# Fourier and attention layers on one core: squares of the shared weight tiles by pieces, separate load buffers, another pace for the modulation

## The chip, the cores and the metric

The kernel runs on one core of a Trainium2 chip. A core has TensorE (PE, matrix products), VectorE (DVE), ScalarE (ACT), GpSimd (POOL) and SyncE (SP, which only issues transfers here). The metric is the device time of one execution in microseconds (us); lower is better.

## The reference

Two layers work on 256 tokens and 256 context tokens of width 2048. Layer 0 mixes by a Fourier transform, layer 1 by attention. Each has a modulation (shift, scale, gate) out of `c`, and an output product `y @ w_out`.

```python
def _fourier_branch(h, w_in, w_mix):
    b, n, _ = h.shape
    u, z = jnp.split(h @ w_in, 2, axis=-1)
    ug = u.reshape(b, n, FNET_GROUPS, FNET_GROUP_DIM).astype(jnp.float32)
    f = jnp.fft.fft2(ug, axes=(1, 3), norm='ortho').real.astype(h.dtype)
    f = jnp.einsum('bngc,gcd->bngd', f, w_mix).reshape(b, n, D_BRANCH)
    return f * jax.nn.silu(z)
...
    for i in range(DEPTH):
        shift, scale, gate = jnp.split((jax.nn.silu(c) @ ada_w[i] + ada_b[i])[:, None, :], 3, axis=-1)
        h = _rmsnorm(x, norm_g[i]) * (1 + scale) + shift
        if need_ctx or kind == 1:
            shift_c, scale_c, gate_c = jnp.split(jax.nn.silu(c_ctx) @ ada_w[i] + ada_b[i], 3)
            hc = _rmsnorm(xc, norm_g[i]) * (1 + scale_c) + shift_c
        if kind == 0:
            y = _fourier_branch(h, fnet_w_in[j], fnet_w_mix[j])
            yc = _fourier_branch(hc, fnet_w_in[j], fnet_w_mix[j]) if need_ctx else None
        elif kind == 1:
            y, yc = _attention_branch(h, hc, attn_w_in[j], attn_sink[j], rows, cols, need_ctx)
...
        x = x + gate * (y @ w_out[i])
        if need_ctx:
            xc = xc + gate_c * (yc @ w_out[i])
    return _rmsnorm(x, final_g)
```

## The kernel before

Tokens and context tokens are handled together, as 512 columns. The stages in order of time, with the profile's times:

- **Opening** (to some 120 us): norm, modulation of layer 0, and the Fourier transform over the tokens.
- **u-stage** (to some 337 us): 16 groups `g` of the Fourier branch. For each group two tiles `wu` of 1 MB come from memory, are folded on DVE (L134, L140), split into a high and a low part on ACT (L66) and DVE (L67), and multiplied with the tokens held in 32 `act` tiles; the mix matrix `m` comes through ACT's queue. The result `ft` goes to a table `fd` in memory.
- **z-stage** (to some 672 us): the other half of `w_in`. The first four output blocks, b = 0 to 3, share four tiles `wz0` (one per four k, loop over `kg`); each of blocks 4 to 31 has a tile `wz` of its own. A tile is first squared and summed over (`squares`, L161), the sum gives a scale (`total` on POOL, `scale`), and then it is split into two half-precision tiles `w16` (`split16`: ACT L179, then DVE L180). A block is 48 matmuls: 16 k, three products each (L79, L80, L81). The tokens `hs` are built anew for each k by `make_hs` (DVE L768, ACT L769, DVE L770). `z_out` takes the Silu of the block (ACT L779) and multiplies it with the branch tile `ys[b]`, read back from `fd`.
- **Output product of layer 0, wo0** (to some 1008 us): 32 tiles, n = 0 to 31, each 48 matmuls again, in the order of the list `outs`. `y_split` makes the halves of y; `evac0` scales the result by `gd`, the gate times the tile's scale, and adds it to x.
- **Layer 1**: attention, to the end.

Beside the z-stage and wo0 run the 64 **modulation steps** (`ada_step`): a step loads one tile `adw` of 1 MB and forms four sums on DVE (L730, output `junk`), two for the last 16 steps. The `cb` vectors they use have their Silu on ACT (L723).

The order of the work on each engine is not written by hand. A scheduler takes the program's order, the buffers of the pools and hints (`tc.issue_after`) and fixes one sequence for each engine; an engine then takes its instructions strictly in that sequence. So a buffer that is not free, or an instruction whose input is late, holds back all that follows on its engine or queue. All loads of weights go through SP's queue.

The pools that matter: `rawp` with three buffers of 1 MB (`raw`); `zp`, three more (`rawz`), whose memory is free only after the u-stage's pools have closed; `wsp` with six buffers for split weights; `actp` with 33 buffers, of which the tokens take 32 in the u-stage; eight PSUM banks. `raw6` takes `raw` and `rawz` in turn, for weights and `adw` alike. `fetch(n)` loads, squares and scales tile n; `weights(n)` splits it and calls `fetch(n + 2)`.

Of the kernel before, what the change touches and what calls it, by code (L numbers as in the profile page):

```python
# [32 lines left out]
def tile_dit(ctx: ExitStack, tc: tile.TileContext, a: dict, out: bass.AP):  # L33
# [13 lines left out]
    def raw(src, q=None):  # L47
        t = rawp.tile([P, D], F32, tag="raw", name="raw")
        n = src.shape[-1]
        last_dma[0] = (q or nc.sync).dma_start(t[:, :n], src).ins  # L50
        return t
# [108 lines left out]
    def squares(dump, src, col, scale=1.0):  # L160
        sq_ins[0] = S.activation(dump, src, AF.Square, scale=scale, accum_out=col).ins  # L161
# [407 lines left out]
        fill_pe(len(fill))  # L569


    w4 = adap.tile([P, 4], F32, name="w4")
    hsc = adap.tile([P, 2, KT, 2], F32, name="hsc")
    hq = [small("hq") for _ in range(3)]
    squares(hsc[:, 0], gs0, hq[0], 64.0)
# [16 lines left out]
    for g in range(G):  # L592
# [36 lines left out]
        if g == 13:  # L629
            w1 = small("w1", bufs=1)  # L630
            V.tensor_reduce(w1, w4, axis=AX.X, op=ALU.add)
            u4, d4 = scale(total(w1), hdn, "4", 1)
        if 8 <= g < 12:
            t = raw(a["wz0"][g - 8])
            squares(t, t, w4[:, g - 8 : g - 7])
        if g > 4:
            with tc.issue_after(m_end[2]):
                w.append({"m": split_part("m", f3[1][1])})
# [99 lines left out]


    adat = lay0.enter_context(tc.tile_pool(name="adat", bufs=1))  # L740
    junk = adat.tile([P, 1056], BF16, name="junk")[:, 0:1024]
    acc = adat.tile([P, 4, 2, KT, 2], F32, name="acc")
    YA = 8
    with tc.tile_pool(name="yp", reuse_waits="tile", bufs=33 - YA) as ypool, tc.tile_pool(name="zp", reuse_waits="tile", bufs=3) as zp:
        ys = [act() if b < YA else ypool.tile([P, 512], F32, tag="y", name="y") for b in range(NB)]
        hs = []
        hs_end = [None] * 3
        turn = [0]

        def raw6(src, view=lambda t, s: ((t, s),)):  # L750
            turn[0] += 1
            pool, nm = (rawp, "raw") if turn[0] % 2 else (zp, "rawz")
            t = pool.tile([P, D], F32, tag=nm, name=nm)
            for d, s in view(t, src):
                last_dma[0] = nc.sync.dma_start(d, s).ins
            return t

        ada_raw = raw6

        def make_hs(k):  # L760
            xt = act()
# [9 lines left out]
            hs.append((hl[:, 0:512], hl[:, 512:1024]))  # L771

        yq = adap.tile([P, NB], F32, name="yq")
        yup, ydn, yy = [None] * 2, [None] * 2, []

        def z_out(b, o, dn):
# [25 lines left out]
        def fetch(n):  # L802
            if n >= len(jobs):
                return
            nm, at_, i = jobs[n]
            if nm == "wz":
                t = raw6(a["wz"][at_])
            else:
                v = a["wo0"][at_[0] // 8, i * 8 : i * 8 + 8].rearrange("g p (j b f) -> p g j b f", j=2, b=8)[:, :, :, at_[0] % 8]
                t = raw6(v, lambda t, s: [(t.rearrange("p (g j f) -> p g j f", g=8, j=2)[:, :, j], s[:, :, j]) for j in range(2)])  # L810
            h, q = half16(), small("wq")
            squares(h, t, q)
            ready[n] = t, h, *scale(total(q), hdn if nm == "wz" else ydn[i])

        def weights(n):
            t, wh, up_, dn = ready.pop(n)
# [4 lines left out]

        o4 = [psum() for _ in range(4)]
        for kg in range(4):
            wr = raw6(a["wz0"][kg])
            wh, wl = half16(), half16()
            for i in range(2):
                make_hs(kg * 4 + i * 2)
                q = slice(i * 1024, (i + 1) * 1024)
                with tc.issue_after(hs_end[0]) if kg else nullcontext(), tc.issue_after(hs_end[1]) if kg else nullcontext():
                    split16(wh[:, q], wl[:, q], wr[:, q], u4)  # L830
                make_hs(kg * 4 + i * 2 + 1)
            for j in range(4):
                k = kg * 4 + j
                for b in range(4):
                    q = slice(j * 512 + b * P, j * 512 + (b + 1) * P)
                    mm3(o4[b], wh[:, q], wl[:, q], hs[k][0], hs[k][1], k == 0, k == KT - 1)
        for b in range(4):
            with tc.issue_after(last_dma[0]):
                nc.sync.dma_start(ys[b], fd[b])
        for b in range(4):  # L840
            z_out(b, o4[b], d4)
        fetch(0)
        fetch(1)
        for b in range(4, NB):
            wh, wl, dn = weights(b - 4)
            with tc.issue_after(last_dma[0]):
                nc.sync.dma_start(ys[b], fd[b])
            o = psum()
            for k in range(KT):
                q = slice(k * P, (k + 1) * P)  # L850
                mm3(o, wh[:, q], wl[:, q], hs[k][0], hs[k][1], k == 0, k == KT - 1)
            z_out(b, o, dn)
            if b == 15:
                y_scale(0)
            if b >= 16:
                y_split()
            with tc.issue_after(hs_end[0]) if b < 8 else nullcontext():
                ada_step(1)
# [4 lines left out]
        def evac0(b, i, o, dn):  # L863
            t = xin[b]
            gd = adap.tile([P, 2], F32, tag="gd", name="gd", bufs=4)
            V.tensor_scalar(gd, gt0[:, b, :], dn, None, op0=ALU.mult)
            t2 = act() if i else None
            for s in range(2):
                q = slice(s * N, (s + 1) * N)
# [19 lines left out]
        for n, (b, i) in enumerate(outs):  # L889
            if n == 0:  # L890
                y_scale(1)
            wh, wl, dn = weights(n + NB - 4)
            if n < 4:
                for _ in range(4):
# [5 lines left out]
            if n == 31:  # L900
                wr = raw(a["wkv"][0])
                w0 = half_split(wr, 0)
            ada_step(0 if n > 29 else 2 if n > 19 else 1)
            o = psum()
            for k in range(16):
                q = slice(k * P, (k + 1) * P)
# [631 lines left out]
```

## Time and profile before

| | us |
|---|---|
| median of 3 runs | 1787.43 (1785.95 to 1788.46) |
| profiled execution | 1785.5 |
| its span | 1783.7 |
| TensorE busy | 1731.1 (97%) |
| VectorE busy | 1398.2 (78%) |
| ScalarE busy | 1039.3 (58%) |

The span is the time from the first to the last recorded instruction of the profiled execution. In rows of waits the columns are: who waited, for whom, us in total, times, longest. In rows of the timeline: start, duration, engine and source line, operation, output<-input, count, and in brackets the idle time before it with the one that ended it. In rows of windows: the stretch, its length, then busy time and instruction count of PE, PEld (weight loads of TensorE), DVE, ACT and POOL, the granted clock of TensorE, the busy share of the DMA engines and GB/s.

### The profile page before, as it was taken

What the parts mean: (1) busy time and instruction counts of PE and PEld (TensorE: products, weight loads), DVE (VectorE), ACT (ScalarE), POOL (GpSimd) and SP (SyncE); (2) the same over time, 40 slices, a digit from 0 to 9 for tenths busy, and PEclk for the clock granted to TensorE, in tenths of its full rate; (3) what the DMA queues carried; (4) which work ended last, traced back from release to release, by engine and by line L of the source; (5) the groups of instructions that cost most, each with busy time, mean ns of one, the idle gap of its engine ahead of it and who ended that gap; (6) DMA issues with size and microseconds to landing.
All of it is one profiled execution on the core that took longest, in us unless ns stands there. A gap on an engine that the chain in (4) does not pass through costs nothing. (4 is left out here: it accounts for less than half of the span.)

```text
span 1783.7 us, 25965 instructions
## 1 busy us (share of the span) xinstructions
PE 1731.1 (97%) x9449; PEld 1204.6 (68%) x9449; DVE 1398.2 (78%) x2415; ACT 1039.3 (58%) x1708; POOL 256.6 (14%) x277
## 2 busy tenths in 40 slices
PE   6999999999999999999999999999999999999997
PEld 4679999644444444444444588788888888887886
DVE  5779778789889997953587463989999999997455
ACT  5544544485565656444334343777888888887343
POOL 0002111211000001100101000322212212234001
PEclk9999999999999999999999999999999999999999
DMA  9998898857777798654468323578898988888554
GB/s 393 417 340 230 234 279 237 288 214 283 275 261 264 259 327 256 204 164 130 131 226 275 112 97 104 174 179 219 213 208 211 216 208 208 210 216 262 197 179 142
DMA packets 267777, 403.06 MB, mean 226 GB/s; under 512 B 152641, under 2 KB 218577, under 8 KB 236161
## 3 DMA queue, kind: packets, MB, share of 16 engines
q1 hardware_dynamic: 243584, 363.39, 64.9%
q0 software_dynamic: 19920, 31.06, 6.9%
q10 hardware_dynamic: 4144, 6.95, 1.2%
q8 instruction: 74, 1.21, 0.3%
q14 instruction: 55, 0.44, 0.1%
HBM read 356.26 MB, written 12.59 MB: 207 GB/s over the span
## 5 line engine op out<-in xcount | busy, mean ns | idle before, releaser
L67 DVE TENSOR_TENSOR wl<-raw,wh 128x1024 fp32r<-128x1024 f32 x205 | 272.3, 1334 | 112.0 <-ACT wh L66 109.3
L66 ACT CAST wh<-raw 128x1024 fp32r<-128x1024 f32 x205 | 214.2, 1046 | 136.9 <-PE ps L80 123.6
L730 DVE CUSTOM_DVE_ANT_0 junk<-rawz,cb 128x1024 bf16<-128x1024 f32 x200 | 244.0, 1220 | 8.5 <-ACT cb L723 5.6
L80 PE MATMUL ps<-act,w 128*128 128x512 f16 x640 | 243.5, 381 | 0.5 <-DVE act L770 0.5
L79 PE MATMUL ps<-act,w 128*128 128x512 f16 x640 | 239.4, 381 | 4.0 <-ACT w L179 2.2
L81 PE MATMUL ps<-act,w 128*128 128x512 f16 x640 | 239.6, 379 | 0.2 <-DVE w L180 0.2
L1203 PE MATMUL ps<-h,wh 128*128 128x512 f32 x512 | 187.1, 403 | 0.0
L81 PEld LDWEIGHTS <-w 128*128 128x128 f16 x1024 | 100.2, 98 | 127.9 <-DVE w L180 6.8
L79 PEld LDWEIGHTS <-w 128*128 128x128 f16 x1024 | 100.4, 98 | 125.2 <-ACT w L179 3.3
L80 PEld LDWEIGHTS <-w 128*128 128x128 f16 x1024 | 100.4, 98 | 120.6 <-issue 0.8
L180 DVE SCALAR_TENSOR_TENSOR w<-raw,up,w 128x2048 f16<-128x2048 f32 (+1 forms) x58 | 131.8, 2274 | 51.5 <-PE ps L80 45.1
L161 ACT ACTIVATE w<-raw 128x2048 f16<-128x2048 f32 x54 | 102.8, 1904 | 94.2 <-PE ps L81 50.0
L81 PE MATMUL ps<-y,w 128*128 128x512 f16 x384 | 145.2, 379 | 4.0 <-DVE w L180 4.0
L80 PE MATMUL ps<-y,w 128*128 128x512 f16 x384 | 145.4, 379 | 0.0
L79 PE MATMUL ps<-y,w 128*128 128x512 f16 x384 | 144.9, 379 | 0.0
L1205 PE MATMUL ps<-h,wl 128*128 128x256 f32 x512 | 138.4, 281 | 0.0
L179 ACT ACTIVATE w<-raw,up 128x2048 f16<-128x2048 f32 (+1 forms) x58 | 112.1, 1935 | 23.3 <-DVE up L170 22.2
L80 PE MATMUL ps<-wl,h 128*128 128x512 f32 x320 | 125.1, 391 | 0.3 <-DVE wl L67 0.3
L81 PE MATMUL ps<-wh,h 128*128 128x512 f32 x320 | 123.8, 390 | 0.0
L79 PE MATMUL ps<-wh,h 128*128 128x512 f32 x320 | 122.4, 397 | 0.0
L165 POOL PARTITION_ALL_REDUCE tot<-wq x60 | 42.6, 713 | 541.5 <-ACT w L161 456.8
L1257 DVE SCALAR_TENSOR_TENSOR f<-p,sm,f 128x512 f16<-128x512 f32 x128 | 103.1, 824 | 12.0 <-ACT f L1256 11.8
(380 smaller groups left out, 4051.7 us busy)
## 6 DMA issues: line engine op xcount, KB each, us to landing
raw<-in_wz SPq DMA_DIRECT2D x65, 1024.0 KB, 5.3
rawz<-in_adw SPq DMA_DIRECT2D x56, 1024.0 KB, 5.1
raw<-in_awp SPq DMA_DIRECT2D x32, 1024.0 KB, 12.8
raw<-in_wq SPq DMA_DIRECT2D x32, 1024.0 KB, 5.2
raw<-in_wu SPq DMA_DIRECT2D x32, 1016.0 KB, 7.3
raw<-in_wo SPq DMA_DIRECT2D x54, 512.0 KB, 5.7
raw<-in_wo1b SPq DMA_DIRECT2D x16, 1024.0 KB, 4.9
act<-in_xT POOLq DMA_DIRECT2D x32, 256.0 KB, 6.3
```

The source lines that it names most:

```text
L66: last_cast[0] = S.copy(h, src).ins
L67: last_sub[0] = eng.tensor_tensor(l, src, h.bitcast(F32), op=ALU.subtract).ins
L79: PE.matmul(o, wh, xh, start=start, stop=False)
L80: PE.matmul(o, wh, xl, start=False, stop=False)
L81: return PE.matmul(o, wl, xh, start=False, stop=stop).ins
L161: sq_ins[0] = S.activation(dump, src, AF.Square, scale=scale, accum_out=col).ins
L179: last_cast[0] = S.activation(h, src, AF.Copy, scale=up).ins
L180: last_sub[0] = V.scalar_tensor_tensor(l, src, up, h, op0=ALU.mult, op1=ALU.subtract).ins
L730: V.tensor_tensor_reduce(junk, wf, cb[:, s], 1.0, 0.0, ALU.mult, ALU.add, acc[:, i, kh, fg * 2 + f, s : s + 1])
L1203: PE.matmul(o[0], wh[:, q], hx1[k], start=k == 0, stop=k == KT - 1)
L1205: PE.matmul(o[0][:, 0:N], wl[:, q], hx1[k][:, 0:N], start=False, stop=False)
L1257: V.scalar_tensor_tensor(f[:, 512:1024], pt[tb], sm[:, tb : tb + 1], f[:, 0:512], op0=ALU.mult, op1=ALU.subtract)
```

## The change

- **Pieces.** In the u-stage the four tiles `wz0` were loaded whole into `raw` at g = 8 to 11, to take the sum of their squares. Now they come as 16 pieces of 128x512, two per group at g = 4 to 11 in the program, each into an `act` tile; `w4` has 16 columns.
- **Buffers.** Weights (`wz0`, `wz`, `wo0`) take only `raw`; the tiles `adw` only `rawz`.
- **Branch tiles.** `ys` are allocated when each is loaded (`load_y`), after the tokens, and nine rather than eight of them lie in `actp`.
- **First squares.** The squares of the first two own tiles, b4 and b5, are issued after the last ACT cast of the tokens (`hs_end[1]`).
- **Gate.** `gty` holds the gate times y's scale for both halves, once; the tiles' `dn` of wo0 are no longer scaled one by one on ACT (L173, 32 times).
- **Pace.** In wo0 the modulation steps were one per n up to n = 19 and two from 20 to 29. Now they are one up to 3, two from 4 to 9, one from 10 to 29. There are 64 in both.

```diff
@@ -569,7 +569,7 @@
         fill_pe(len(fill))
 
 
-    w4 = adap.tile([P, 4], F32, name="w4")
+    w4 = adap.tile([P, 16], F32, name="w4")
     hsc = adap.tile([P, 2, KT, 2], F32, name="hsc")
     hq = [small("hq") for _ in range(3)]
     squares(hsc[:, 0], gs0, hq[0], 64.0)
@@ -630,9 +630,11 @@
             w1 = small("w1", bufs=1)
             V.tensor_reduce(w1, w4, axis=AX.X, op=ALU.add)
             u4, d4 = scale(total(w1), hdn, "4", 1)
-        if 8 <= g < 12:
-            t = raw(a["wz0"][g - 8])
-            squares(t, t, w4[:, g - 8 : g - 7])
+        if 4 <= g < 12:
+            for i in range(g * 2 - 8, g * 2 - 6):
+                t = act()
+                nc.sync.dma_start(t, a["wz0"][i // 4, :, i % 4 * 512 : i % 4 * 512 + 512])
+                squares(t, t, w4[:, i : i + 1])
         if g > 4:
             with tc.issue_after(m_end[2]):
                 w.append({"m": split_part("m", f3[1][1])})
@@ -738,24 +740,30 @@
 
 
     adat = lay0.enter_context(tc.tile_pool(name="adat", bufs=1))
-    junk = adat.tile([P, 1056], BF16, name="junk")[:, 0:1024]
+    junk = adat.tile([P, 1040], BF16, name="junk")[:, 0:1024]
     acc = adat.tile([P, 4, 2, KT, 2], F32, name="acc")
-    YA = 8
+    YA = 9
     with tc.tile_pool(name="yp", reuse_waits="tile", bufs=33 - YA) as ypool, tc.tile_pool(name="zp", reuse_waits="tile", bufs=3) as zp:
-        ys = [act() if b < YA else ypool.tile([P, 512], F32, tag="y", name="y") for b in range(NB)]
+        ys = []
+
+        def load_y(b):
+            ys.append(act() if b < YA else ypool.tile([P, 512], F32, tag="y", name="y"))
+            with tc.issue_after(last_dma[0]):
+                nc.sync.dma_start(ys[b], fd[b])
+
         hs = []
         hs_end = [None] * 3
-        turn = [0]
-
-        def raw6(src, view=lambda t, s: ((t, s),)):
-            turn[0] += 1
-            pool, nm = (rawp, "raw") if turn[0] % 2 else (zp, "rawz")
-            t = pool.tile([P, D], F32, tag=nm, name=nm)
-            for d, s in view(t, src):
-                last_dma[0] = nc.sync.dma_start(d, s).ins
+        def raw_wo(b, i):
+            t = rawp.tile([P, D], F32, tag="raw", name="raw")
+            v = a["wo0"][b // 8, i * 8 : i * 8 + 8].rearrange("g p (j b f) -> p g j b f", j=2, b=8)
+            for j in range(2):
+                last_dma[0] = nc.sync.dma_start(t.rearrange("p (g j f) -> p g j f", g=8, j=2)[:, :, j], v[:, :, j, b % 8]).ins
             return t
 
-        ada_raw = raw6
+        def ada_raw(src):
+            t = zp.tile([P, D], F32, tag="rawz", name="rawz")
+            nc.sync.dma_start(t, src)
+            return t
 
         def make_hs(k):
             xt = act()
@@ -771,6 +779,7 @@
             hs.append((hl[:, 0:512], hl[:, 512:1024]))
 
         yq = adap.tile([P, NB], F32, name="yq")
+        gty = [adap.tile([P, KT, 2], F32, name=f"gty{i}") for i in range(2)]
         yup, ydn, yy = [None] * 2, [None] * 2, []
 
         def z_out(b, o, dn):
@@ -803,14 +812,11 @@
             if n >= len(jobs):
                 return
             nm, at_, i = jobs[n]
-            if nm == "wz":
-                t = raw6(a["wz"][at_])
-            else:
-                v = a["wo0"][at_[0] // 8, i * 8 : i * 8 + 8].rearrange("g p (j b f) -> p g j b f", j=2, b=8)[:, :, :, at_[0] % 8]
-                t = raw6(v, lambda t, s: [(t.rearrange("p (g j f) -> p g j f", g=8, j=2)[:, :, j], s[:, :, j]) for j in range(2)])
+            t = raw(a["wz"][at_]) if nm == "wz" else raw_wo(*at_)
             h, q = half16(), small("wq")
-            squares(h, t, q)
-            ready[n] = t, h, *scale(total(q), hdn if nm == "wz" else ydn[i])
+            with tc.issue_after(hs_end[1]) if n < 2 else nullcontext():
+                squares(h, t, q)
+            ready[n] = t, h, *scale(total(q), hdn if nm == "wz" else None)
 
         def weights(n):
             t, wh, up_, dn = ready.pop(n)
@@ -821,7 +827,7 @@
 
         o4 = [psum() for _ in range(4)]
         for kg in range(4):
-            wr = raw6(a["wz0"][kg])
+            wr = raw(a["wz0"][kg])
             wh, wl = half16(), half16()
             for i in range(2):
                 make_hs(kg * 4 + i * 2)
@@ -835,16 +841,14 @@
                     q = slice(j * 512 + b * P, j * 512 + (b + 1) * P)
                     mm3(o4[b], wh[:, q], wl[:, q], hs[k][0], hs[k][1], k == 0, k == KT - 1)
         for b in range(4):
-            with tc.issue_after(last_dma[0]):
-                nc.sync.dma_start(ys[b], fd[b])
+            load_y(b)
         for b in range(4):
             z_out(b, o4[b], d4)
         fetch(0)
         fetch(1)
         for b in range(4, NB):
             wh, wl, dn = weights(b - 4)
-            with tc.issue_after(last_dma[0]):
-                nc.sync.dma_start(ys[b], fd[b])
+            load_y(b)
             o = psum()
             for k in range(KT):
                 q = slice(k * P, (k + 1) * P)
@@ -863,7 +867,7 @@
         def evac0(b, i, o, dn):
             t = xin[b]
             gd = adap.tile([P, 2], F32, tag="gd", name="gd", bufs=4)
-            V.tensor_scalar(gd, gt0[:, b, :], dn, None, op0=ALU.mult)
+            V.tensor_scalar(gd, gty[i][:, b, :], dn, None, op0=ALU.mult)
             t2 = act() if i else None
             for s in range(2):
                 q = slice(s * N, (s + 1) * N)
@@ -889,6 +893,8 @@
         for n, (b, i) in enumerate(outs):
             if n == 0:
                 y_scale(1)
+                for d, y in zip(gty, ydn):
+                    V.tensor_scalar(d, gt0, y, None, op0=ALU.mult)
             wh, wl, dn = weights(n + NB - 4)
             if n < 4:
                 for _ in range(4):
@@ -900,7 +906,7 @@
             if n == 31:
                 wr = raw(a["wkv"][0])
                 w0 = half_split(wr, 0)
-            ada_step(0 if n > 29 else 2 if n > 19 else 1)
+            ada_step(1 if n < 4 or 9 < n < 30 else 2 if n < 10 else 0)
             o = psum()
             for k in range(16):
                 q = slice(k * P, (k + 1) * P)
```

On SP, in the u-stage: `raw<-in_wz` are the whole shared tiles, `act<-in_wz` the pieces, `raw<-in_wu` the loads of the groups. Before:

```order
L50 DMA raw<-in_wz 128x2048 [waits DMAHW7_49,DMASW0_49,DVE_49]
L50 DMA raw<-in_wu 128x2032 [waits DMAHW6_49,Activation_49]
L50 DMA raw<-in_wu 128x2032 [waits DMAHW2_49,DVE_49]
L50 DMA raw<-in_wz 128x2048 [waits DMAHW0_49,DMAHW3_49,DMASW3_49,DVE_49]
L50 DMA raw<-in_wu 128x2032 [waits Activation_49]
L50 DMA raw<-in_wu 128x2032 [waits DMAHW6_49,DVE_49]
```

After:

```order
L50 DMA raw<-in_wu 128x2032 [waits DMAHW5_49,DVE_49]
L636 DMA act<-in_wz 128x512 [waits DMAHW6_49,Activation_49]
L636 DMA act<-in_wz 128x512 [waits DMAHW1_49,Activation_49]
L636 DMA act<-in_wz 128x512 [waits DMAHW2_49,Activation_49]
L636 DMA act<-in_wz 128x512 [waits DMAHW3_49,Activation_49]
L50 DMA raw<-in_wu 128x2032 [waits DMAHW5_49,DMASW0_49,DVE_49]
L636 DMA act<-in_wz 128x512 [waits DMAHW6_49,Activation_49]
L50 DMA raw<-in_wu 128x2032 [waits DMAHW7_49,DMAHW0_49,DVE_49]
```

The loads of whole tiles are gone from between the group's loads, together with the waits for ACT behind them; pieces that wait for ACT stand there now, the first of them ahead of the first `wu` load.

On ACT, at the end of the shared product. Before, w16_4540 and w16_4552 are tiles b4 and b5, w16_4428 is the last shared tile, and L769 are the casts of tokens:

```order
L161 ACTIVATE w16_4540,wq_4541<-raw_4538 128x2048 [waits DMAHW3_49,PE_49,Activation_49]
L161 ACTIVATE w16_4552,wq_4553<-rawz_4550 128x2048 [waits DMAHW3_49,PE_49]
L769 ACTIVATE act_4443<-act_4441,hsc_1404 128x256 [waits DMASW4_49,DVE_49]
L769 ACTIVATE act_4443<-act_4441,hsc_1404 128x256 [waits DVE_49]
L179 ACTIVATE w16_4540<-raw_4538,up_4545 128x2048 [waits DVE_49,Activation_49]
L173 ACTIVATE dn_4546<-dn_4546,dnh_1414 128x1 [waits DVE_49]
L179 ACTIVATE w16_4552<-rawz_4550,up_4557 128x2048 [waits DVE_49,Activation_49]
L769 ACTIVATE act_4452<-act_4450,hsc_1404 128x256 [waits DMASW5_49,DVE_49]
L769 ACTIVATE act_4452<-act_4450,hsc_1404 128x256 [waits DVE_49]
L179 ACTIVATE w16_4428<-rawz_4426,up4_3534 128x1024
```

After, w16_4550 and w16_4562 are b4 and b5, ps_4152 to ps_4155 the four blocks of the shared product, L777 the last cast of tokens, L725 the Silu of `cb` and L788 those of the blocks:

```order
L777 ACTIVATE act_4469<-act_4467,hsc_1404 128x256 [waits DVE_49]
L161 ACTIVATE w16_4550,wq_4551<-raw_4548 128x2048 [waits DMAHW0_49,PE_49,Activation_49]
L161 ACTIVATE w16_4562,wq_4563<-raw_4560 128x2048 [waits DMAHW1_49,PE_49]
L725 ACTIVATE cb_4642<-cb_4642 128x2048 [waits DMASW7_49]
L788 ACTIVATE act_4532<-ps_4152,dn4_3571 128x512 [waits PE_49]
L788 ACTIVATE act_4536<-ps_4153,dn4_3571 128x512 [waits PE_49]
L788 ACTIVATE act_4540<-ps_4154,dn4_3571 128x512 [waits PE_49]
L179 ACTIVATE w16_4550<-raw_4548,up_4555 128x2048 [waits DVE_49,Activation_49]
L173 ACTIVATE dn_4556<-dn_4556,dnh_1414 128x1 [waits DVE_49]
L788 ACTIVATE act_4544<-ps_4155,dn4_3571 128x512 [waits PE_49]
L179 ACTIVATE w16_4562<-raw_4560,up_4567 128x2048 [waits DVE_49,Activation_49]
```

Squares and splits of b4 and b5 stood among the casts of tokens; now both squares stand behind the last cast, and the splits behind three and four of the Silus, which wait for TensorE.

On TensorE at the same place, with the same names. Before, the first matmuls of b4 and b5 stand ahead of the shared product's second half of its last tile:

```order
L79 LDWEIGHTS w16_4540 [waits Activation_49]
L79 MATMUL ps_4578<-act_4156,w16_4540 128x512
L80 LDWEIGHTS w16_4540
L80 MATMUL ps_4578<-act_4156,w16_4540 128x512
L79 LDWEIGHTS w16_4552 [waits Activation_49]
L79 MATMUL ps_4656<-act_4156,w16_4552 128x512
```

After, they follow its last matmul (ps_4155, k = 15):

```order
L80 MATMUL ps_4155<-act_4469,w16_4434 128x512
L81 LDWEIGHTS w16_4435
L81 MATMUL ps_4155<-act_4469,w16_4435 128x512
L79 LDWEIGHTS w16_4550 [waits Activation_49]
L79 MATMUL ps_4589<-act_4162,w16_4550 128x512
L80 LDWEIGHTS w16_4550
L80 MATMUL ps_4589<-act_4162,w16_4550 128x512
L79 LDWEIGHTS w16_4562 [waits Activation_49]
```

The matmuls of b4, and then the weights of b5, thus come directly behind the shared product. On DVE, 11 sums and 7 halves of y stand between the splits of tiles n = 5 and n = 6 of wo0, where 10 and 5 stood before.

## The prediction

> **What bounds the kernel now.** I read the page first, then TensorE's waits by stage, then the queue or engine behind each wait, then the granted clock beside it. The page says that TensorE is the bound almost throughout:
>
> ```profile
> span 1783.7 us, 25965 instructions
> PE 1731.1 (97%) x9449; PEld 1204.6 (68%) x9449; DVE 1398.2 (78%) x2415; ACT 1039.3 (58%) x1708; POOL 256.6 (14%) x277
> ```
>
> No matmul is added or removed, so only TensorE's idle time (1783.7 - 1731.1 = 52.6 us) and its slow clock can change; the opening and layer 1, which hold most of that, keep their order. The waits of TensorE in the three touched stretches, u-stage (200 to 285 us), the passage from the shared tiles to tile b4 (330 to 380), and the first output product with the end of the z-stage (640 to 1010):
>
> ```profile
> PE ps L79 <- ACT mh L66: 5.8, 2, 3.7
> PE ps L79 <- ACT ft L700: 1.2, 1, 1.2
> ```
>
> ```profile
> PE ps L79 <- ACT w L179: 2.2, 1, 2.2
> PE ps L79 <- ACT act L769: 1.6, 1, 1.6
> ...
> PE ps L80 <- DVE act L770: 0.5, 1, 0.5
> ```
>
> ```profile
> PE ps L81 <- DVE w L180: 4.2, 4, 1.5
> ```
>
> So 7.0, 4.3 and 4.2 us. Two of the gaps also leave a slow clock behind them; the windows just after the longest gaps (PEclk, the granted clock, is the third figure from the right):
>
> ```profile
> 240.00:245.00 5.00, 5.00 (x31) 5.00 (x31) 3.01 (x4) 0.91 (x1) 0.00 (x0) 0.66 1.17 283
> 345.00:350.00 5.00, 3.14 (x8) 1.20 (x9) 2.98 (x6) 2.05 (x3) 0.00 (x0) 0.68 0.47 148
> 735.00:740.00 5.00, 3.50 (x17) 1.44 (x16) 5.00 (x6) 0.63 (x1) 2.31 (x1) 1.00 0.33 95
> ```
>
> In the first, 5 x (1 - 0.66) = 1.7 us is lost on top of the gap, in the second 5 x (1 - 0.68) = 1.6; behind the 1.5 us gap of the third nothing is. Before, the three stretches lose 7.0 + 1.7 = 8.7, 4.3 + 1.6 = 5.9 and 4.2 us.
>
> **Part 1, the sixteen pieces.** Why the u-stage waits is read from SP's queue:
>
> ```profile
> 196.81 0.33 SPq L50 DMA_DIRECT2D raw<-in_wz  x1
> 204.29 2.51 SPq L50 DMA_DIRECT2D raw<-in_wu  x2
> 209.91 0.33 SPq L50 DMA_DIRECT2D raw<-in_wz  x1
> 220.77 3.88 SPq L50 DMA_DIRECT2D raw<-in_wu  x2
> 231.24 0.33 SPq L50 DMA_DIRECT2D raw<-in_wz  x1
> ```
>
> Each shared tile takes one of the three `raw` buffers, and the next `wu` loads go only when its square has been taken. Two answers name the consequence: SP waits for the square, and VectorE's fold waits for the late load (both from 190 to 275 us):
>
> ```profile
> SPq L50 <- ACT raw L161: 13.8, 2, 7.1
> ```
>
> ```profile
> DVE wm L134 <- DMA raw<-in_wu: 8.7, 4, 3.0
> ```
>
> The four tiles leave `raw`, so I take the whole 8.7 us as gained. Bounds: nothing, if VectorE's fullness and not the load makes the gaps (it folds and subtracts for 61.3 of 70 us, row below), and 8.7.
>
> What the pieces cost: 16 squares of 512 elements, 16 issues on SP of 0.33 us, in place of four squares of 1.9 us. The bandwidth is the same. But every piece uses the same 33rd `act` buffer, so piece i+1 is issued only after square i, and `wu` loads stand behind it on SP; and on ScalarE a square that is reached before its piece has landed holds back the casts behind it. A load of this size and its queue's neighbours (115 to 215 us), and the load of the engines (140 to 210):
>
> ```profile
> raw<-in_wu SPq DMA_DIRECT2D x12, 1016.0 KB, 6.6
> ...
> m<-in_wm ACTq DMA_DIRECT2D x7, 256.0 KB, 3.2
> ```
>
> ```profile
> 140.00:210.00 70.00, 70.00 (x583) 70.00 (x583) 61.34 (x90) 37.38 (x68) 12.98 (x15) 1.00 0.90 246
> ```
>
> A round trip is 3.2 us, plus the issue; where two squares have only one to four casts of about 1 us between them, ScalarE waits some 2 us for the second. I find three such places, around 134 to 144 us, some 5 to 6 us of ScalarE, which has 70 - 37.4 = 32.6 us to spare; VectorE behind it has 8.7. I take 0.5 us of TensorE, between 0 and 9 (1.5 for each of six groups).
>
> **Part 2, separate buffers and the new order at tile b4.** Before, `wz0` tile 1 came into a `rawz` buffer that did not exist until the u-stage's pool closed; that is the wait of 4.1 us here (335 to 372 us), and TensorE's 2.2 with its slow clock:
>
> ```profile
> L179 ACT ACTIVATE w<-rawz,up 128x1024 f16<-128x1024 f32 x3 | 3.4, 1137 | 4.1 <-DMA rawz<-in_wz 4.1
> ```
>
> It goes: all four now use `raw`, free at the end of the u-stage. The 1.6 and 0.5 us go too, since they come from the squares of b4 and b5 (the first row below is one) that stood among the last casts of tokens, and these squares now wait for the last cast. But that is where the new wait is. ScalarE before:
>
> ```profile
> 368.90 1.90 ACT L161 ACTIVATE w<-raw 128x2048 f16<-128x2048 f32 x1
> ...
> 373.49 1.99 ACT L179 ACTIVATE w<-raw,up 128x2048 f16<-128x2048 f32 x1
> ...
> 381.37 0.89 ACT L769 ACTIVATE act<-act,hsc 128x256 f16<-128x256 f32 x2
> 382.17 1.89 ACT L723 ACTIVATE cb<-cb 128x2048 f32<-128x2048 f32 x1
> ...
> 387.53 2.42 ACT L779 ACTIVATE act<-ps,dn 128x512 f32<-128x512 f32 x4 [1.39 <-PE ps L81]
> ```
>
> The last cast of tokens (L769) ends at 382.3. From 368.90 on three squares and two splits of tiles stand ahead of it, 3 x 1.9 + 2 x 2.0 = 9.7 us; without them it ends at 372.6, and with VectorE's part of the chain I take 373. TensorE's rate in this arithmetic:
>
> ```profile
> 744.00:940.00 196.00, 196.00 (x909) 88.83 (x908) 117.78 (x205) 85.26 (x87) 14.49 (x27) 1.00 0.57 168
> ```
>
> 196 / 909 = 0.216 us a matmul, 12 of them for a k of the shared product, 2.6 us: it ends at about 375.6. In the new order ScalarE then has the squares of b4 and b5 (3.8), the `cb` Silu (1.8), and three of the four Silus of the product (2.42 / 4 = 0.6 each, 1.8) ahead of b4's split (2.0): 373 + 9.4 = 382.4 us. TensorE has nothing else in its order, so it stands for 382.4 - 375.6 = 6.8 us. After two matmuls of b4 comes b5's weight load, whose split follows one more scale and Silu: (0.6 + 2.0) - 2 x 0.216 = 2.2 us more. With the slow clock that followed the long gaps, 1.7, that makes 10.7 against 5.9 before: +4.8. Before, matmuls of b4 and b5 were ahead of the last two k and covered this. Bounds: 0, if TensorE reaches the product's end so late that only the three Silus and the split are left ahead of it (1.8 + 2.0 + 2.2 = 6.0 us and no slow clock), and +7, if ScalarE is 2 us later than 373.
>
> [...]
>
> **Part 3, the pace of the modulation steps.** A step is four reductions, and VectorE does them between the splits. Before (716.23 and 734.72 are the splits of n = 5 and 6 of the output product):
>
> ```profile
> 716.23 2.35 DVE L180 SCALAR_TENSOR_TENSOR w<-raw,up,w 128x2048 f16<-128x2048 f32 x1
> ...
> 727.30 0.74 DVE L180 SCALAR_TENSOR_TENSOR y<-y,upy,y 128x512 f16<-128x512 f32 x1
> 727.97 1.22 DVE L730 CUSTOM_DVE_ANT_0 junk<-rawz,cb 128x1024 bf16<-128x1024 f32 x1
> ...
> 734.72 2.35 DVE L180 SCALAR_TENSOR_TENSOR w<-raw,up,w 128x2048 f16<-128x2048 f32 x1
> ```
>
> ```profile
> 672.00:744.00 72.00, 70.50 (x327) 31.83 (x326) 64.61 (x110) 39.30 (x46) 8.92 (x11) 1.00 0.71 228
> ```
>
> From split to split 18.5 us passed, against 48 x 0.216 = 10.4 us of matmuls for one n; the lead that VectorE had was used up, and TensorE waited 1.5 us. In the new order 11 reductions and 7 halves of y stand between the two, instead of 10 and 5: 1.22 + 2 x 0.67 (from 727.30 to 727.97) = 2.6 us more. Ahead of them, from n = 1 to 5, the new order has about the work of the old, and VectorE, which idled for 72 - 64.6 = 7.4 us in this stretch, most of it around n = 1 and 2, may get there up to 1.9 us earlier, as reductions now stand where it idled. I take +2 (a wait of 3.5), between +0.7 and +4.3, the 2.6 with a slow clock of 1.7 behind it. From n = 7 on each n has 10 to 12 us of VectorE's work, a lead of some 6 us, and no wait; from n = 17 only 3.5. The two steps per n that stood at n = 20 to 29 are gone, and with them the rest of the 4.2: -2.7.
>
> The 32 scalings of `dn` on ScalarE that go, and the later allocation of y, I count at nothing: in the row from 744 to 940 ScalarE is idle for 196 - 85 = 111 us and VectorE for 78, and TensorE never. Without that cover 32 short instructions would count.
>
> **Sum.** -8.7 + 0.5 + 4.8 + 2 - 2.7 = -4.1 us. Against the profiled execution, 1785.5 us, of which 1.8 lie around the span: 1781.4. The median shown is 1.9 higher, so 1783.3 us.
>
> **Rivals.**
> - *The passage shrinks to its floor.* If TensorE ends the shared product some 3 us later than 375.6 for a reason that does not hold back ScalarE, the loss is 6.0 us, what it was before. The sum is then -8.9, and -10.2 with the lower bound of part 3: 1777 to 1778.5. For it: I rebuilt that chain from one trace. Against it: the chain that feeds TensorE's last k is the one that ScalarE follows. Chance 0.22.
> - *The pieces' ring stalls (slower).* One buffer, a round trip of 3.2 us and more when 1 MB loads of 6.6 us run beside it; `wu` loads wait on SP behind each piece. From the point at which a piece lands some 3 us after ScalarE has reached its square, VectorE's 8.7 spare us per 70 are gone and each of six groups loses about 1.5 us: +9 in place of +0.5, in all +4.4: 1792. Against it: pieces are spread over ten groups and ScalarE has half its time free. Chance 0.23.
> - *The u-stage does not gain what its waits show.* VectorE at 61.3 of 70 us is near the bound; if the gaps close only half, 4.3 us fewer: 1787.6, no change. For it: that row leaves little room. Against: VectorE itself waits 8.7 us for `wu` there, so it had that room. Chance 0.15.
>
> **How the numbers follow.** The forecast itself, 1781 to 1786, has 0.40. A measurement of this kernel can tell some 0.2%, 3.6 us, from no change; the forecast is -4.1, so 0.26 of it count as faster and 0.14 as no change. With the rivals: faster 0.26 + 0.22 = 0.48; same 0.14 + 0.11 = 0.25; slower 0.23 + 0.04 = 0.27. The range for 8 in 10 takes in the passage that closes and the ring: 1774 to 1794; the forecast's own is 1779 to 1788.
>
> **What would show it.** Right: TensorE's waits on `mh` and `ft` between 200 and 285 us gone, no wait on `raw` by SP there; one wait on ScalarE's split of 6 to 7 us and another of 2 to 3 where the shared product ends, with a granted clock well under 1 for the window after; a wait of some 3.5 us on VectorE's split about 60 us into the output product, and none after it. Wrong: waits on ScalarE's casts between 130 and 200 us (the ring), a `wu` fold still late, or the passage without a gap.

## The result, and the profile after

The changed kernel takes 1795.55 us (median of 5 runs, 1794.26 to 1797.73) against 1787.43 us: 1.0049 times the time before, 95% interval 1.0034 to 1.0063. It is slower, by half a percent, and slower than the range of the forecast (1774 to 1794). Forecast were 1783.3 us, 4.1 us less than before.

The page of the changed kernel:

```profile
span 1792.5 us, 25986 instructions
## 1 busy us (share of the span) xinstructions
PE 1735.1 (97%) x9449; PEld 1207.1 (67%) x9449; DVE 1391.3 (78%) x2417; ACT 1036.2 (58%) x1700; POOL 278.6 (16%) x277
```

The span is 8.8 us longer, with as many matmuls. To say where, I compare the start times of three pieces of work in the two traces: the mix of group g = 13 (at 308 us before; only two more groups of the u-stage follow), the Silu of block b = 28 (the passage lies between, with those two groups in it; from b5 on the z-stage keeps its distance) and the last but one tile's evacuation (end of the output product). Each column is the change of a stage's length against the kernel before, in us; the experiments below stand in the same table.

| kernel | u-stage, to g = 13 | from there past b4 | output product | layer 1 | span |
|---|---|---|---|---|---|
| forecast | -8.2 | +4.8 | -0.7 | 0 | -4.1 |
| changed kernel | +3.0 | +2.2 | +3.8 | -0.1 | +8.8 |
| e1 pieces alone | +4.6 | -1.8 | 0.0 | +1.9 | +4.7 |
| e2 squares paced | -8.4 | +3.5 | +4.6 | +4.3 | +3.9 |
| e3 no hint at b4 | +1.9 | -4.0 | -3.0 | -0.1 | -5.2 |
| e4 old pace | +1.2 | +3.3 | +4.3 | +0.8 | +9.6 |
| e5 pieces on ScalarE's queue | 0.0 | +2.0 | +4.0 | +1.5 | +7.5 |
| e6 steps held | +0.1 | +3.0 | -3.5 | +2.8 | +2.4 |
| e7 paced, no hint | -8.9 | -5.7 | -2.6 | +5.4 | -11.8 |
| e8 the same, steps held | -9.4 | -4.4 | -0.6 | +2.0 | -12.4 |
| e9 shared buffers | +1.3 | +6.6 | -5.0 | -0.3 | +2.6 |
| e10 e7 with the old pace | -9.7 | -5.8 | -1.0 | +4.6 | -11.8 |
| e11 e7 with shared buffers | -8.6 | -4.4 | -5.0 | +0.1 | -18.0 |

Each row is one profiled execution. Two pairs of rows have the same order of work on every engine, the changed kernel and e4, and e7 and e10: between them the columns differ by up to 1.8 us, and differences of that size are not read here. Layer 1 has the same order in all rows but e1, e8 and e11, where it differs a little at its start, and still its column runs from -0.1 to +5.4; so the last two columns say little about the change.

TensorE's waits in the changed kernel, in the windows 120 to 215, 330 to 420 and 640 to 1020 us:

```profile
PE ps L79 <- ACT ft L702: 6.6, 3, 3.3
```

```profile
PE ps L79 <- ACT w L179: 8.1, 2, 6.5
```

```profile
PE ps L81 <- DVE w L180: 6.4, 2, 5.8
```

The waits of before in the u-stage are gone, between 205 and 290 us TensorE does not wait. But there are new ones of 3.3 us at 132 us and 3.0 us at 182 us, on ScalarE's copies into `ft`. What ScalarE waits for there (110 to 215 us), and what it looks like (a stretch of its timeline):

```profile
ACT act L161 <- DMA act<-in_wz: 35.8, 13, 3.9
```

```profile
137.94 0.63 ACT L161 ACTIVATE act<-act 128x512 f32<-128x512 f32 x1 [1.43 <-DMA act<-in_wz]
...
138.57 0.56 ACT L66 CAST pqh<-ps 128x512 fp32r<-128x512 f32 x1
139.04 0.47 ACT L456 ACTIVATE sp<-ps,mk 96x256 fp32r<-96x256 f32 x1
141.77 0.63 ACT L161 ACTIVATE act<-act 128x512 f32<-128x512 f32 x1 [2.26 <-DMA act<-in_wz]
...
142.49 1.06 ACT L66 CAST wph<-raw 128x1016 fp32r<-128x1016 f32 x1
146.09 0.64 ACT L161 ACTIVATE act<-act 128x512 f32<-128x512 f32 x1 [2.54 <-DMA act<-in_wz]
```

The squares (L161) stand one to three short instructions apart; each waits for its piece, and the casts and copies behind it wait with it. SP, in turn, can issue the next piece only after the square of the last (110 to 300 us):

```profile
SPq L636 <- ACT act L161: 39.3, 9, 6.6
```

By the eighth group the kernel is 12.4 us behind the one before. From 120 to 215 us TensorE's waits come to 6.9 us, and the granted clock under 1 takes another 5.1, added up over windows of 5 us as the prediction does; before, 0.2 and nothing. Up to the twelfth group it makes up 9.4, where the other had its whole-tile waits. The clock after the gaps (PEclk third from the right):

```profile
135.00:140.00 5.00, 4.53 (x26) 4.53 (x27) 3.72 (x7) 2.80 (x10) 0.00 (x0) 0.70 0.50 173
...
185.00:190.00 5.00, 4.79 (x21) 4.51 (x22) 2.94 (x3) 1.40 (x4) 1.05 (x2) 0.50 0.98 169
383.00:388.00 5.00, 2.71 (x6) 0.71 (x7) 5.00 (x7) 5.00 (x10) 0.00 (x0) 0.50 0.17 25
...
745.00:750.00 5.00, 2.57 (x7) 0.92 (x8) 5.00 (x6) 0.63 (x1) 0.00 (x0) 0.50 0.33 102
```

ScalarE at the end of the shared product, in the order that the prediction laid out:

```profile
373.51 0.91 ACT L777 ACTIVATE act<-act,hsc 128x256 f16<-128x256 f32 x2 [1.75 <-DVE act L776]
374.32 1.90 ACT L161 ACTIVATE w<-raw 128x2048 f16<-128x2048 f32 x1
...
378.11 1.89 ACT L725 ACTIVATE cb<-cb 128x2048 f32<-128x2048 f32 x1
379.91 1.81 ACT L788 ACTIVATE act<-ps,dn 128x512 f32<-128x512 f32 x3
381.62 2.00 ACT L179 ACTIVATE w<-raw,up 128x2048 f16<-128x2048 f32 x1
...
384.26 2.00 ACT L179 ACTIVATE w<-raw,up 128x2048 f16<-128x2048 f32 x1
```

And VectorE's longest wait between 660 and 750 us; before, VectorE does not wait for `cb` in this stretch:

```profile
DVE junk L732 <- ACT cb L725: 8.7, 1, 8.7
```

### The profile page after: what moved, and what is told of

The parts are those of the page before. It is cut to its first block, busy times and chain, and to the rows that moved or that the text cites. A ratio compares the mean times of both kernels' runs of the same rounds, so it can differ in the third digit from the quotient of the medians.

```text
span 1792.5 us, 25986 instructions
## 1 busy us (share of the span) xinstructions
PE 1735.1 (97%) x9449; PEld 1207.1 (67%) x9449; DVE 1391.3 (78%) x2417; ACT 1036.2 (58%) x1700; POOL 278.6 (16%) x277
## 5 line engine op out<-in xcount | busy, mean ns | idle before, releaser
L732 DVE CUSTOM_DVE_ANT_0 junk<-rawz,cb 128x1024 bf16<-128x1024 f32 x224 | 273.6, 1221 | 26.0 <-ACT cb L725 23.2
L79 PE MATMUL ps<-act,w 128*128 128x512 f16 x656 | 245.4, 381 | 8.1 <-ACT w L179 8.1
L80 PE MATMUL ps<-act,w 128*128 128x512 f16 x656 | 249.5, 380 | 0.0
L81 PE MATMUL ps<-act,w 128*128 128x512 f16 x656 | 246.0, 380 | 0.0
L180 DVE SCALAR_TENSOR_TENSOR w<-raw,up,w 128x2048 f16<-128x2048 f32 (+1 forms) x68 | 151.1, 2223 | 91.7 <-PE ps L80 88.3
L161 ACT ACTIVATE w<-raw 128x2048 f16<-128x2048 f32 x60 | 114.4, 1906 | 107.9 <-PE ps L81 69.0
L179 ACT ACTIVATE w<-raw,up 128x2048 f16<-128x2048 f32 (+1 forms) x68 | 128.5, 1895 | 38.0 <-DVE up L170 37.2
L81 PE MATMUL ps<-y,w 128*128 128x512 f16 x368 | 139.6, 381 | 6.4 <-DVE w L180 6.4
L165 POOL PARTITION_ALL_REDUCE tot<-wq x60 | 62.0, 1037 | 515.8 <-ACT w L161 441.9
L80 PE MATMUL ps<-y,w 128*128 128x512 f16 x368 | 139.8, 381 | 0.0
L79 PE MATMUL ps<-y,w 128*128 128x512 f16 x368 | 139.3, 381 | 0.0
```

Source lines behind the costliest of these rows:

```text
L79: PE.matmul(o, wh, xh, start=start, stop=False)
L80: PE.matmul(o, wh, xl, start=False, stop=False)
L81: return PE.matmul(o, wl, xh, start=False, stop=stop).ins
L179: last_cast[0] = S.activation(h, src, AF.Copy, scale=up).ins
L180: last_sub[0] = V.scalar_tensor_tensor(l, src, up, h, op0=ALU.mult, op1=ALU.subtract).ins
L732: V.tensor_tensor_reduce(junk, wf, cb[:, s], 1.0, 0.0, ALU.mult, ALU.add, acc[:, i, kh, fg * 2 + f, s : s + 1])
```

## The experiments

Theory R: ScalarE, which takes its work in order, waits for each piece's round trip through one buffer. Rival S: the loads of `wu` behind the pieces on SP are late. Theory J: the hint at b4 makes the passage's gap; rival K: the chain of the tokens is the bound there. For the output product, P: the new pace fills VectorE; Q: the modulation steps' own buffers let them be drawn forward whatever the pace.

**e1, the kernel before with the pieces alone**

```diff
-        if 8 <= g < 12:
-            t = raw(a["wz0"][g - 8])
-            squares(t, t, w4[:, g - 8 : g - 7])
+        if 4 <= g < 12:
+            for i in range(g * 2 - 8, g * 2 - 6):
+                t = act()
+                nc.sync.dma_start(t, a["wz0"][i // 4, :, i % 4 * 512 : i % 4 * 512 + 512])
+                squares(t, t, w4[:, i : i + 1])
```

> The kernel before with only the sixteen pieces (and a narrower junk tile, so that the memory suffices); buffers, branch tiles, first squares, gate and pace as before. Theory R (ScalarE, strictly in order, waits for each piece's round trip through the one 33rd buffer): the changed kernel's trace loses 12.4 us by its eighth group and regains 9.4 by the twelfth, so the u-stage ends 3.0 us later than before and the rest is as before: some +3 us, 1790.5. Rival B (the u-stage's loss in the changed kernel comes from the other edits, by another order): then the pieces alone take away the waits for the whole tiles, -8 us, 1779.

The trace agrees with R: ScalarE waits 37.4 us for pieces, the kernel is 14 us behind by the eighth group and 4.6 at g = 13. But this execution was the slowest of ten; the median is 1786.57 us against 1789.19, ratio 0.9985 (0.9971 to 0.9998). R's +3 is outside this interval, and B's -8 is too. So the pieces by themselves about break even: the traces with unpaced pieces have a u-stage 0 to 4.6 us longer than before, the median of this run is 2.6 us shorter. The gain of 8.2 us that was forecast for them is excluded.

**e2, the squares paced**

```diff
+        def piece(i, end):
+            t = act()
+            nc.sync.dma_start(t, a["wz0"][i // 4, :, i % 4 * 512 : i % 4 * 512 + 512])
+            with tc.issue_after(end):
+                squares(t, t, w4[:, i : i + 1])
...
         split(mh[0:127, :, 1:128], ml[0:127, :, 1:128], oa["m"][:, :, 1:128])
+        if 4 <= g < 12:
+            piece(g * 2 - 8, last_cast[0])
...
         evacs.append((last_cast[0], last_sub[0]))
+        if 4 <= g < 12:
+            piece(g * 2 - 7, last_cast[0])
```

> The changed kernel, but each square of a piece is placed behind a named cast of its own group, two per group in groups 4 to 11, some 7 us apart, so that the next piece has that long to come. Theory R: ScalarE's 35.8 us of waits for pieces fall under 5 us, the two 3 us gaps of TensorE at 132 and 182 us vanish, and the whole-tile gaps stay away: 9 to 12 us faster than the change, some 1784 to 1786. Rival S (it is the loads of wu behind the pieces on SP that come late, not the squares on ScalarE): as many pieces stand in SP's queue, the folds still wait, and the gain is under 3 us.

ScalarE's waits for pieces fall from 35.8 to 4.5 us (110 to 270 us), and what is left of TensorE's waits from 120 to 335 us is

```profile
PE ps L80 <- DVE ml L67: 0.9, 1, 0.9
PE ps L79 <- ACT ft L708: 0.3, 1, 0.3
```

The u-stage is 8.4 us shorter than before, 11.4 than in the changed kernel. R holds. The whole, 1787.91 us or 0.9994 (0.9981 to 1.0007), misses the expected 1784 to 1786: the passage and the output product keep their losses, and layer 1 took 4.3 us more in this execution (last section).

**e5, the pieces on ScalarE's own queue**

```diff
-                nc.sync.dma_start(t, a["wz0"][i // 4, :, i % 4 * 512 : i % 4 * 512 + 512])
+                nc.scalar.dma_start(t, a["wz0"][i // 4, :, i % 4 * 512 : i % 4 * 512 + 512])
```

> The changed kernel with the sixteen pieces loaded through ScalarE's queue instead of SP's. Theory R (ScalarE waits in order for each piece): the pieces are awaited as before, some 30 to 40 us of ScalarE's time, the gaps of TensorE at 132 and 182 us stay; the time is the changed kernel's within 3 us, 1793 to 1798. Rival S (the wu loads behind the pieces on SP are late): SP is free of pieces, the u-stage has no gaps, 8 to 11 us faster, 1785 to 1787.

1796.46 us, 1.0046 (1.0031 to 1.0062): the changed kernel's time. With SP free of pieces ScalarE still waits for them, though for less than I expected:

```profile
ACT act L161 <- DMA act<-in_wz: 22.4, 12, 4.1
```

TensorE's waits from 120 to 335 us come to 5.9 us, the longest 1.6, against 6.9 and 3.3 in the changed kernel. S, which asked for no gaps and 8 to 11 us, falls: it is the squares in the first place. That the pieces on SP cost a microsecond or two besides is not excluded.

**e3, no hint at b4**

```diff
-            with tc.issue_after(hs_end[1]) if n < 2 else nullcontext():
-                squares(h, t, q)
+            squares(h, t, q)
```

> The changed kernel without the hint that holds the squares of b4 and b5 behind the last cast of the tokens. Theory J (that hint makes the passage's gap): matmuls of b4 and b5 stand ahead of the shared product's end again, the gaps of 6.45 and 1.62 us and the slow clock after them (1.7) go, and waits of some 2 us on the tokens' casts, as before the change, come back: about -6 to -7.5 us against the change, 1788 to 1789.5. Rival K (the chain of the tokens is the bound, and the squares put into it delay TensorE as much): -2 us or less.

1783.10 us, 0.9969 (0.9953 to 0.9984), faster than before, with the ring of pieces still in it, and some 5 us under the 1788 to 1789.5 expected. The passage's waits (330 to 400 us):

```profile
PE ps L79 <- ACT act L777: 1.5, 1, 1.5
PE ps L80 <- DVE act L778: 0.5, 1, 0.5
PE ps L79 <- ACT mh L66: 0.4, 1, 0.4
```

J holds: 6.2 us of the passage come back. The rest is a second effect that I had not expected. The wait in the output product falls from 6.4 to 1.9 us, and VectorE's wait for the Silu of `cb` is gone: without the hint the scheduler puts the fourth `cb` later.

**e4, the old pace**

```diff
-            ada_step(1 if n < 4 or 9 < n < 30 else 2 if n < 10 else 0)
+            ada_step(0 if n > 29 else 2 if n > 19 else 1)
```

> The changed kernel with the pace of before for the modulation steps in the output product. Theory P (the two steps per n from 4 to 9 fill VectorE and make the 5.84 us wait at n = 6): that wait falls to some 1.5 us, the later waits of 2.7 us come back, about -4 us, 1791.5. Rival Q (the steps' own three buffers let them be drawn forward to n = 0 to 6 whatever the pace, and there VectorE waits 8.7 us for the Silu of the next cb): the wait at n = 6 stays near 5.8, the later waits come back, 0 to +3 us, 1795.5 to 1798.5.

1795.11 us, 1.0036 (1.0020 to 1.0052). The waits of the output product are the changed kernel's, to the tenth:

```profile
PE ps L81 <- DVE w L180: 6.4, 2, 5.8
```

P falls. The late waits that Q expected back did not come either. With buffers of their own the steps are drawn forward so far that all are done by the split of n = 16, and the scheduler arrives at the same order on every engine with either pace: this run is a repeat of the changed kernel.

**e6, the steps held**

```diff
             wh, wl, dn = weights(n + NB - 4)
+            if n == 2:
+                n2 = last_sub[0]
...
-            ada_step(1 if n < 4 or 9 < n < 30 else 2 if n < 10 else 0)
+            with tc.issue_after(n2) if n > 3 else nullcontext():
+                ada_step(1 if n < 4 or 9 < n < 30 else 2 if n < 10 else 0)
```

> The changed kernel, with the modulation steps of n = 4 and later held behind VectorE's split of n = 2; nothing else moves. In the new order no sums stand between the splits of n = 0 to 2, where VectorE waited 8.7 us for the fourth cb, and four to six stand between any two later ones. Theory Q (that wait, and the eleven sums drawn forward to before n = 6, make TensorE's 0.6 and 5.84 us waits and the slow clock after): no wait over 0.3 us on VectorE's split, 7 to 8.5 us faster than the change: 1787 to 1788.5. Rival P (two steps per n from 4 to 9 are too many in any order): a wait of 3 us or more comes at n = 7 to 12, gain under 4 us.

1788.74 us, 1.0010 (0.9994 to 1.0026), against 1795.55 of the changed kernel. The output product is 7.2 us shorter. One wait of 1.4 us is left at n = 6, against an expected 0.3 at most. VectorE waits 4.5 us for the fourth `cb` just ahead of that split. The program's two steps per n that P blamed do not show in the order: at most six sums stand between two splits.

**e9, the buffers shared again**

```diff
-        def ada_raw(src):
-            t = zp.tile([P, D], F32, tag="rawz", name="rawz")
+        def raw6(src, view=lambda t, s: ((t, s),)):
+            turn[0] += 1
+            pool, nm = (rawp, "raw") if turn[0] % 2 else (zp, "rawz")
+            t = pool.tile([P, D], F32, tag=nm, name=nm)
...
-            wr = raw(a["wz0"][kg])
+            wr = raw6(a["wz0"][kg])
```

> The changed kernel with raw and rawz taken in turn again by weights and modulation tiles (the new pace, the pieces, the hint and the gate stay). In its order VectorE has 3 to 11 us of work between any two splits of the output product, and the fourth cb is first used at n = 5. Theory Q2 (it is the steps' own three buffers that let them be drawn forward; with shared buffers the new pace spreads them): no wait on VectorE's split in the output product, 7 to 8 us regained there; the passage has the hint's gaps, and the load of wz0 tile 1 into rawz is late again, 2 to 4 us lost: 3 to 6 us faster than the change, 1790 to 1792.5. Rival P2 (own buffers do not matter there): the 5.84 us wait stays, slower than the change by 2 to 4 us.

1793.09 us, 1.0027 (1.0012 to 1.0042), just above the expected band. No wait at all on VectorE's split in the output product, 5.0 us less than before there: Q2 holds. In the passage the wait for the tile in `rawz` is back beside the hint's two (330 to 400 us):

```profile
PE ps L79 <- ACT w L179: 10.2, 4, 6.5
```

**e7 and e8, the two cures together, and the steps held as well.** e7 has e2's and e3's edits, e8 those of e6 too.

> The changed kernel with the paced squares and without the hint at b4 and b5. If the two causes are independent, the sum of their stages: u-stage 8.4 us earlier than before, the passage 4 us better than before, the output product 3 us better: 15 to 16 us faster than before, ratio 0.991 to 0.992. If a faster u-stage only moves the wait to the passage (the wz0 tiles or the tokens' loads come late): 8 to 11 us.

> The same with the modulation steps held as well: no wait on VectorE's split in the output product. Another 1.9 us less than the paced kernel without the hint, 17 to 18 us faster than before, ratio 0.990. If holding the steps only moves VectorE's work to the start of layer 1: no difference to that kernel.

e7: 1770.94 us, 0.9902 (0.9880 to 0.9924), 16.8 us less than before. The two causes add up: by the ratios e2 is 9.8 us and e3 14.3 us faster than the changed kernel, e7 26.3 us. e8: 1768.48 us, 0.9889 (0.9863 to 0.9915); the intervals overlap, and in the trace a wait of 2.6 us at n = 6 remains where none was expected, behind VectorE's wait of 5.6 us for the fourth `cb` just ahead of that split. So what holding adds here stays open.

**e10, e7 with the old pace**

> The kernel with paced squares and no hint, with the old pace of the steps. Its order on VectorE is the same as with the new pace up to n = 16. Theory Q2 (with own buffers the buffers, not the pace, say when a step runs): the same time within 2 us, ratio to before 0.989 to 0.992. Rival P: waits of some 2.7 us at n = 26 to 29 as before the change, ratio 0.9915 to 0.993.

1774.38 us, 0.9910 (0.9885 to 0.9934), inside Q2's band; no waits came back at n = 26 to 29. The order is that of e7 on every engine, so this is a second measurement of e7, and the 3.4 us between the two medians show how far two such runs lie apart.

**e11, e7 with the later buffers shared.** The shared tiles `wz0` keep `raw`; `wz`, `wo0` and the modulation tiles take turns as in e9.

> The kernel with paced squares and no hint, where the shared tiles wz0 use raw alone, but all later weights and the modulation tiles take raw and rawz in turn, with the new pace. Theory Q2: as in e9 no wait on VectorE's split in the output product, and the passage as without the hint; the 2.3 us wait at n = 6 of that kernel goes: 17 to 19 us faster than before, ratio 0.989 to 0.9905. Rival: b5 comes into rawz, whose memory is free only after the u-stage's pools, and the passage waits for it, 2 to 4 us lost: ratio 0.9915 or more.

1769.23 us, 0.9883 (0.9859 to 0.9906), 19.3 us less than before; its interval overlaps those of e7, e8 and e10. The page:

```profile
span 1765.7 us, 25971 instructions
...
PE 1726.4 (98%) x9449; PEld 1202.4 (68%) x9449; DVE 1396.0 (79%) x2417; ACT 1036.2 (59%) x1700; POOL 258.9 (15%) x277
```

TensorE does not wait for VectorE's split anywhere in the output product. From 695 to 745 us, some n = 3 to 8, it is busy without a break, where the changed kernel (690 to 745 us, some n = 1 to 6) has VectorE full and TensorE not:

```profile
695.00:745.00 50.00, 50.00 (x233) 22.70 (x232) 37.71 (x66) 25.69 (x23) 3.21 (x6) 1.00 0.82 268
```

```profile
690.00:745.00 55.00, 50.99 (x236) 22.67 (x233) 54.90 (x99) 30.77 (x31) 5.13 (x5) 1.00 0.63 203
```

VectorE still waits 5.0 us for the fourth `cb` in e11, and TensorE does not notice: here the wait falls between the splits of n = 8 and 9, with three sums. In e8 it fell just ahead of the split of n = 6, and TensorE lost 2.6 us; in the changed kernel it came at n = 1, with eleven sums in one place behind it, and TensorE lost 5.8. In e3 ten sums stand in that place without the wait, and TensorE lost 1.9. So the pile of sums costs some 2 us by itself, and the wait comes on top where VectorE has no lead left.

## Why the prediction was wrong

Forecast and profile lie some 13 us apart in the span (-4.1 and +8.8): 11.2 of it in the u-stage, -2.6 in the passage, 4.5 in the output product.

- **The whole tiles' waits (-8.7): right.** The changed kernel regains 9.4 us from the eighth to the twelfth group, and with the squares paced the kernel is 8.4 to 9.7 us ahead at g = 13. The third rival, VectorE's fullness, is refuted by the same number.
- **The pieces (+0.5): the step that failed.** It measured 12.4 us up to the eighth group. Three terms were wrong. The round trip was taken as 3.2 us from the neighbouring loads; between 115 and 215 us it was

```profile
raw<-in_wu SPq DMA_DIRECT2D x11, 1016.0 KB, 6.8
act<-in_wz SPq DMA_DIRECT2D x15, 256.0 KB, 4.8
...
m<-in_wm ACTq DMA_DIRECT2D x7, 256.0 KB, 4.1
```

  The places counted were three, and there were thirteen: each late square makes the next load late too, so the ring never gets ahead, and the pieces, reckoned over ten groups, were all issued between 109 and 197 us, by the seventh group. ScalarE waited 35.8 us, not 5 to 6. And its 32.6 spare us of 70 were set against that: its spare time is no cover for a copy that TensorE needs in this group. My second rival had the ring's stall, though by way of VectorE's spare time, and priced it at +9, in all 1792, with a chance of 0.23. That this is near the 1795.55 measured is in part luck: the stall cost 12.4, and the errors of the other two stages partly cancel.
- **The passage (+4.8): the gaps right, the net too high.** 6.8 and 2.2 us were forecast, 6.45 and 1.62 measured, one behind the split of b4 and one behind that of b5, and the clock fell to 0.50 (383 to 388 us). The net was +2.2. Of the 2.6 between, 1.6 were gained before the last group's mix: a wait of 1.1 us on `mh` near 331 us, which the sum left out, belongs there and went as well. The rest I cannot divide.
- **The output product (+2 and -2.7): wrong in sign and cause.** The step that failed is that VectorE "may get there up to 1.9 us earlier, as reductions now stand where it idled". The first of these sums needs the fourth `cb`, which shares a buffer with the third: its load was issued at 667.1 us, after the last sum with the third had begun at 665.6, and landed 9.7 us later; VectorE stood for 8.7 us and came to n = 6 late by 5.8. I had read the order, but not that one row in it waited for a load of 9.7 us. And the pace, to which I put the whole part, does nothing here: in e4 and e10 the old pace gives the same order, so the steps' own buffers say when a step runs; e9 and e11, with shared buffers, have no wait on the split, and e6, with the steps held, one of 1.4 us. The late waits of 2.7 us did go, but not through the pace.
- **The gate and y's allocation (0): not tested by themselves.** e11 keeps both and shows no wait of TensorE on them in the output product.

## What to carry to other kernels

An engine with half its time free can still be the bound when it takes its work in order and a load stands in it: ScalarE, busy for 58% of the span, stood for 35.8 us at the pieces, and by the eighth group the kernel was 12.4 us behind. Count the round trip at the load of that moment (here 4.8 us, where 3.2 was taken), and ask whether the ring of buffers can ever get ahead of its reader. Splitting a load into small ones saves the big buffer and multiplies the number of places where an engine waits (ScalarE waited thirteen times for the sixteen pieces); put each use a round trip behind the previous one (in e2 the 35.8 us fell to 4.5). A buffer taken out of a shared pool moves more than its own loads: whatever it held back (here the modulation steps) is now drawn forward, and the new first place of each stalled load has to be looked at (with the buffers shared again, in e9, the 6.4 us of waits on VectorE's split are gone).

## What the runs showed that I had not expected

- The granted clock fell after gaps of 2 to 3 us too, but not after all of them, and the length of the gap alone does not tell which. After 3.3 and 3.0 us it fell to 0.70 and 0.50 (rows above), after 2.6 us in e8 to 0.66, after 2.3 us in e7 not at all. The rows of e8 and e7, the 5 us behind the gap:

```profile
724.30:729.30 5.00, 4.95 (x16) 1.93 (x17) 5.00 (x9) 0.63 (x1) 0.00 (x0) 0.66 0.74 201
```

```profile
723.30:728.30 5.00, 5.00 (x24) 2.29 (x25) 5.00 (x9) 0.63 (x1) 0.19 (x1) 1.00 1.03 335
```

In the kernel before it was 0.68 from 345 to 350 us, around a gap of 2.2 us (the prediction shows both), and 1.00 behind one of 2.12 us:

```profile
272.56 0.39 PE L79 MATMUL ps<-mh,ch 128*128 128x256 f32 x1 [2.12 <-ACT mh L66]
```

```profile
272.50:277.50 5.00, 4.95 (x42) 4.95 (x42) 4.98 (x8) 2.36 (x6) 0.96 (x2) 1.00 1.08 168
```

- So a small wait can cost twice, or once. In e2 layer 1, where the order does not differ, lost some 4 us near 1630 us against the kernel before: TensorE's waits of 0.5 and 0.9 us from 1610 to 1632 us became 1.4, 1.1 and 1.7, and the granted clock was 0.81 and 0.85 there, against 1.00. e7 and e10 lose as much at the same place; why is open. Single executions of one kernel lie up to 14 us apart (the kernel before: 1781.07 to 1795.30 us in one comparison); that is why I read stages and waits beside the medians.
- A hint that orders two squares at 374 us also changed the first use of the fourth `cb` at 670 us: with it that load is awaited, without it (e3) not.
